# A decoder layer on one core: the position bias moved behind S5's first tables, stores issued by ScalarE, double buffers in the gated unit, and pieces of the merge and of the first FFN products in another order

## The chip, the cores and the metric

The kernel runs on one core of one Trainium2 chip. The metric is the time of one execution in device microseconds. Before the change the median of three runs is 1618.14 us (1615.76 to 1625.18). The profiled execution, from which all rows come, took 1624.46 us.

## What is computed

One layer for a sequence of 1024 tokens with 1024 features, all in float32:

```python
h = rmsnorm(x, norm_mix_g)
u, q, kc_r, vc_r, ks_r, vs_r, kw_r, vw_r, g_nsa, g_br = split(h @ w_in)
y_a = s5_mixer(u, ...) @ w_up_ssm          # recurrence with 64 states per group, then z * sigmoid(z @ w_glu)
kc, vc = compress(kc_r, ...), compress(vc_r, ...)
y_b = nsa_mixer(qh, kc, vc, ks_r, vs_r, kw_r, vw_r, gates, rel_bias) @ w_up_nsa
g_a, g_b = split(sigmoid(g_br))
x = x + (g_a * y_a + g_b * y_b) @ w_out
h = rmsnorm(x, norm_ffn_g)
x = x + (silu(h @ w_ffn_gate) * (h @ w_ffn_up)) @ w_ffn_down
return rmsnorm(x, norm_final_g)
```

The attention adds a position bias of 32 buckets and 8 heads to its logits.

## The kernel before

Every large product is made of three products of 128x512: operands are split into a high part in a reduced format (`wh`, `hhi`, `zh`) and the rest (`wl`, `hlo`, `zl`), and high by high, high by low and low by high are added up in PSUM. The split (`split`, L410) is a cast on ScalarE, GpSimd or VectorE, line 413, 415 or 417, and a subtraction, line 418. Each engine works through its instructions in the order in which the program writes them; that order is the whole schedule. Tiles come from pools with a fixed number of buffers, and a new tile waits until the last user of its buffer is done.

Weights come through `Weights`: two raw buffers (`wr`, loaded by SyncE, L83) and three pairs of split buffers (`wh`, `wl`). `next` (L103) hands out the next unit, and `ahead(2, 4)` splits two and loads four units ahead.

PSUM has the banks "a" (four), "b" and "c" (two each). In attention it is divided anew.

The stages:

1. `head` (L500): the first norm, the transposes of h, the values' projections.
2. `in_proj` (L592), a generator: 28 column blocks of `w_in`, each in two halves of 512 tokens, each half of 8 steps of three products into an "a" bank. What becomes of a bank depends on its kind: "u" (input of S5) goes through eight small copies, "c" (for the compression) and "g" (gates) are copied or passed through the sigmoid by ScalarE (L614, L616), "q" and "k" are split by ScalarE (L607) and VectorE (L608). Then they are stored to DRAM by SyncE (L609, L610, L617). The buffers `evf`, `evh`, `evl` are two each.
3. Beside it runs side work. `along(side, rate)` in `program` takes one piece of the side work (up to its next `yield`) and then `rate` steps of the projections. The side work is, in this order, `s5_params` (rate 4.6), `s5` (3.2), `compress` (3.0) and `glu` (0.8); what is left of the projections comes at the end.
4. `s5_params` (L666) computes the recurrence's parameters in a long chain of small VectorE operations, with the position bias ahead of that chain: 8 products of 128x384 (L712), copies by ScalarE and VectorE, 8 stores. `s5` (L839) works in 8 batches of 4 groups: `tables` on GpSimd and ScalarE (L835, L859), `ways_in` (L873 to L875, giving `w`), `ways_out` (L884 to L890, giving `r`), then transposes, products and a scan.
5. `compress` (L971) loads keys and values (`kk`), eight pieces of 512 KB of its weights (`w1`, L995; three buffers), and multiplies them in groups of 8 small products for each half (L1023). Behind the first three pieces `z_loads` (L1086) loads the input of the gated unit.
6. `glu` (L1057): for each half of the tokens four splits of `z` into `zh` and `zl`, then four products with `w_glu`, a sigmoid (`sg`), a product by VectorE, a split into `ahi` and `alo`.
7. `up_a` (L1093), 16 parts of 12 products, each read from its bank by VectorE (L1110); 12 of them ahead of attention, 4 among its first units. `attention` (L1194) starts a unit (16 rows of a table of due times for each pair of blocks) with `scores` (L1214) and `biased` (L1249).
8. `up_b` and `merge` (L1450): the product with `w_out`, in `units(tiles, half, between)`; each goes over four weight units u, and `between` names what else is written behind or, with "m", in the middle of each u. `square`, `root` and `norm` make the second norm (L1481, L432, L1488), `turned` and `turn("transpose", tile)` its transposes (L469, L1510). For tiles 4 to 7 `turn` also makes sums and differences of the transposed blocks (`sums`, T1, B22, T3, T2, T4; L1517 to L1534).
9. The FFN: `Winograd` replaces each product of 2x2 blocks by seven products of sums of blocks. `pair` (t1 to t4) splits the weights' blocks, `sums` adds them up. `first` (L260) makes the first two weight matrices' products while tiles 6 and 7 are still being normed. Then `run` and the product with `w_ffn_down`.

Of the kernel before, what the change touches and what calls it, by code (L numbers as in the profile page):

```python
# [8 lines left out]
F32 = mybir.dt.float32  # L9
# [7 lines left out]
P = 128  # L17
# [105 lines left out]
class Winograd:  # L123
# [136 lines left out]
    def first(self, norms, turn):  # L260

        V, AC, GP, bank = self.K.nc.vector, self.K.nc.scalar, self.K.nc.gpsimd, self.K.bank
        x0, x1 = self.x[0], self.x[1] = bank("a"), bank("a")
        self.product(0, 1, x0)
        self.product(1, 1, x1)
        next(norms)
        self.t2(0)
        next(norms)  # L270
        self.p1out(0)
        z5 = bank("a")
        self.product(0, 5, z5, half=0)
        turn("transpose", 6, "bc")
        next(norms)
        self.p1out(1)
        turn("sums", 6)
        y = bank("b")
        self.product(0, 6, y, half=0)
        self.product(0, 2, x0, first=False)  # L280
        turn("transpose", 7, "ac")
        turn("T1", 6)
        self.t3(0)
        turn("sums", 7)
        self.product(1, 2, x1, first=False)
        self.p2out(0)
        turn("T1", 7)
        self.t4(0)
        z3, v, c = (bank(t) for t in "abc")
        self.product(0, 3, z3, half=0)  # L290
        self.product(0, 7, v, half=0)
        self.product(0, 4, c, half=0)
        turn("B22", 6)
        turn("B22", 7)
        self.load(2)
        self.product(0, 5, z5, half=1)
        turn("T3", 6)
        turn("T3", 7)
        self.p2out(1)
        self.product(0, 3, z3, half=1)  # L300
        turn("T2", 6)
        turn("T2", 7)
        self.product(0, 7, v, half=1)
        turn("T4", 6)
        turn("T4", 7)
        u2, p5, u3 = self.p.pop(0), self.tile("p1"), self.tile("x11")
        self.product(0, 6, y, half=1)
        self.sums(1, V)
        self.t4(1)
        self.load(3)  # L310
        self.t2(1)
        AC.copy(p5, z5)
        V.tensor_tensor(u2, u2, y, op=OP.add)
        V.tensor_tensor(u3, u2, v, op=OP.add)
        V.tensor_tensor(u2, u2, z3, op=OP.add)
        GP.tensor_tensor(u2, u2, p5, op=OP.add)
        GP.tensor_tensor(p5, u3, p5, op=OP.add)
        self.product(0, 4, c, half=1)
        self.out(0, 1, 1, p5)
        self.out(0, 0, 1, u2)  # L320
        V.tensor_tensor(u3, u3, c, op=OP.add)
        self.out(0, 1, 0, u3)
# [56 lines left out]
class Kernel:  # L379
# [212 lines left out]
    def in_proj(self, specs, ev):  # L592

        nc = self.nc
        for c0, kind, dst in specs:
            w = self.W.next("w_in", 0, KD, c0, P)
            for h in range(2):
# [5 lines left out]
                elif kind in "qk":  # L603
# [5 lines left out]
                    nc.sync.dma_start(dst[0][:, tok], a.bitcast(F32))  # L609
                    nc.sync.dma_start(dst[1][:, tok], b.bitcast(F32))  # L610
                else:
# [5 lines left out]
                    nc.sync.dma_start(dst[:, tok], a)  # L617
# [20 lines left out]
    def s5_loads(self):  # L638
# [22 lines left out]
        self.rb = x("rb", 32, 8)  # L661
        dma(self.rb, A["rel_bias"])
        self.oh = x("oh", 32, 384)
        dma(self.oh, A["consts"][0:32, 874:1258])

    def s5_params(self):  # L666
# [39 lines left out]

        rbb = x("rbb", 32, 8, P)
        V.tensor_copy(rbb, self.rb[:, :, None].to_broadcast([32, 8, P]))
        yield
        for h in range(8):  # L710
            b = self.bank("c")
            nc.tensor.matmul(b[:, 0:384], rbb[:, h, :], self.oh, start=True, stop=True)  # L712
            s = tmp.tile([P, 384], F32, name="brs", tag="brs", bufs=2)
            (AC.copy if h % 2 else V.tensor_copy)(s, b[:, 0:384])
            nc.sync.dma_start(self.bd[h], s)
            yield
# [90 lines left out]
        V.tensor_tensor(self.Bq, self.Bq, w, op=OP.subtract)  # L807

# [29 lines left out]
    def s5(self):  # L838
# [63 lines left out]
        yield  # L902
        zb = None
# [67 lines left out]
    def compress(self, pool):  # L971
# [20 lines left out]
        def w1(j):  # L992
            w = pool.tile([P, 4, 256], F32, name="w1", tag="w1", bufs=3)
# [4 lines left out]
        ws = [w1(j) for j in range(3)]  # L998
# [18 lines left out]
        for which in range(2):  # L1017
            t = self.bank("c")
            for j in range(4):
# [6 lines left out]
                if 4 * which + j < 5:  # L1026
                    ws.append(w1(4 * which + j + 3))
# [29 lines left out]
    def glu(self, pool):  # L1057
        nc, V = self.nc, self.nc.vector
        for h in range(2):
            t = slice(512 * h, 512 * h + 512)  # L1060
            z = self.z[h]
            zs = [pool.tile([P, 4, 512], FR, name=n, tag=n) for n in ("zh", "zl")]
            for k in range(4):
                self.split(zs[0][:, k, :], zs[1][:, k, :], z[:, k, :], "act", "dve")
                yield
            yield
            yield
# [126 lines left out]
    def attention(self, pools, loads, up):  # L1194
# [163 lines left out]
        def start(n):  # L1358
            if n == 2:
# [16 lines left out]
            if n == 1:  # L1376
                run(up, 1)
# [72 lines left out]
    def merge(self, pool, m, td, xd, ffn):  # L1450
# [90 lines left out]
        def units(tts, q, between):  # L1541

            banks = [self.bank("a") for _ in tts]
            for u in range(4):
# [13 lines left out]
                for f, *a in between.get(u, ()):  # L1558
                    f(*a)

        T = lambda tt, *what: [(turn, w, tt) for w in what]
        units((0, 1, 4, 5), 0, {(0, "m"): [(load, tt) for tt in (0, 1, 4, 5)] + [(ffn.factors,)],
# [3 lines left out]
                          1: [(turned, 0)] + T(4, "transpose", "sums"), 2: T(4, "T1", "B22")})  # L1566
# [3 lines left out]
                                (2, "m"): [(load, 6), (load, 7)] + T(5, "T1", "B22"), 2: T(5, "T3", "T2"),  # L1570
                                (3, "m"): T(5, "T4")})
        units((2, 3), 1, {})
# [90 lines left out]
    def program(self):  # L1663
# [25 lines left out]
        self.ut = up.tile([P, G, P], F32, name="ut")  # L1689

# [21 lines left out]
        along(self.s5(), 3.2)  # L1712
        up.release()
# [30 lines left out]
        run(up, 2)  # L1744
# [132 lines left out]
```

## Time and profile before

| | |
|---|---|
| median of three runs | 1618.14 us |
| profiled execution, its own time | 1624.46 us |
| its span, from the first to the last instruction | 1622.7 us |
| TensorE busy | 1561.6 us, 96% |
| VectorE, ScalarE, GpSimd busy | 926.8, 634.6, 637.6 us |
| mean granted TensorE clock | 0.979 of full speed |
| DMA queues' packets | 196.38 MB, mean 121 GB/s |

In the rows PE is TensorE, PEld its weight loads, DVE VectorE, ACT ScalarE, POOL GpSimd and SP SyncE; an engine's name with a q is its queue of DMA issues. L12 is line 12 of the kernel before. Times are microseconds from the span's start. Behind "<-" in square brackets, or after "waited for", stands what ended an engine's idle time, by the semaphores. Ends of matmuls are modelled, and neighbouring ones overlap in the rows.

### The profile page before, as it was taken

What the parts mean: (1) busy time and instruction counts of PE and PEld (TensorE: products, weight loads), DVE (VectorE), ACT (ScalarE), POOL (GpSimd) and SP (SyncE); (2) the same over time, 40 slices, a digit from 0 to 9 for tenths busy, and PEclk for the clock granted to TensorE, in tenths of its full rate; (3) what the DMA queues carried; (4) which work ended last, traced back from release to release, by engine and by line L of the source; (5) the groups of instructions that cost most, each with busy time, mean ns of one, the idle gap of its engine ahead of it and who ended that gap; (6) DMA issues with size and microseconds to landing.
All of it is one profiled execution on the core that took longest, in us unless ns stands there. A gap on an engine that the chain in (4) does not pass through costs nothing. (4 is left out here: it accounts for less than half of the span.)

```text
span 1622.7 us, 22419 instructions
## 1 busy us (share of the span) xinstructions
PE 1561.6 (96%) x7928; PEld 1310.4 (81%) x7928; DVE 926.8 (57%) x1744; ACT 634.6 (39%) x1277; POOL 637.6 (39%) x740
## 2 busy tenths in 40 slices
PE   8998999998999999999999899999999999999995
PEld 8876888886877899998787777888888888888884
DVE  7346886632245899998857564444444445335433
ACT  5212334421220698898116543332333333233322
POOL 1005777610021455555450038677776661000001
PEclk9999999999999999999999989999999999999998
DMA  6342443339337712100666512223222214454551
GB/s 220 107 146 86 123 130 96 94 87 252 98 112 240 203 30 68 42 27 16 217 197 199 176 46 80 89 79 95 81 79 90 79 52 171 150 205 150 177 198 53
DMA packets 165607, 196.38 MB, mean 121 GB/s; under 512 B 20730, under 2 KB 119446, under 8 KB 165495
## 3 DMA queue, kind: packets, MB, share of 16 engines
q1 hardware_dynamic: 165495, 194.94, 38.7%
q8 instruction: 63, 1.03, 0.3%
q14 instruction: 49, 0.40, 0.1%
HBM read 144.96 MB, written 47.84 MB: 119 GB/s over the span
## 5 line engine op out<-in xcount | busy, mean ns | idle before, releaser
L418 DVE TENSOR_TENSOR wl<-wr,wh 128x1024 fp32r<-128x1024 f32 (+1 forms) x170 | 196.8, 1168 | 144.8 <-ACT wh L415 109.6
L406 PE MATMUL a<-hhi,wh 128*128 128x512 f32 x448 | 182.9, 408 | 0.0
L408 PE MATMUL a<-hhi,wl 128*128 128x512 f32 x448 | 178.0, 397 | 0.0
L407 PE MATMUL a<-hlo,wh 128*128 128x512 f32 x448 | 177.8, 397 | 0.0
L415 ACT CAST wh<-wr 128x1024 fp32r<-128x1024 f32 (+1 forms) x138 | 114.4, 844 | 157.2 <-PE a L220 41.6
L1285 POOL TENSOR_SCALAR P<-P,sum,gates 128x640 f32<-128x640 f32 (+3 forms) x192 | 124.8, 663 | 116.6 <-DVE sum L1279 73.5
L219 PE MATMUL a<-mhi,wh 128*128 128x512 f32 (+1 forms) x360 | 139.1, 386 | 2.2 <-ACT wh L415 1.8
L221 PE MATMUL a<-mhi,wl 128*128 128x512 f32 (+1 forms) x360 | 138.7, 385 | 0.8 <-DVE wl L418 0.8
L220 PE MATMUL a<-mlo,wh 128*128 128x512 f32 (+1 forms) x360 | 138.6, 385 | 0.0
L413 POOL TENSOR_SCALAR wh<-wr 128x1024 fp32r<-128x1024 f32 x32 | 34.0, 1064 | 226.8 <-PE a L407 168.8
L160 POOL TENSOR_SCALAR wr<-wr,gcol 128x256 f32<-128x256 f32 x176 | 92.7, 546 | 72.2 <-DVE mlo L474 67.9
L1314 DVE TENSOR_TENSOR PTl<-T,PTh 128x512 fp32r<-128x512 f32 (+3 forms) x200 | 104.2, 544 | 9.7 <-ACT PTh L1313 7.8
L406 PEld LDWEIGHTS a<-hhi,wh 128*128 128x128 f32 x448 | 85.0, 190 | 24.1 <-issue 6.2
L1265 ACT ACTIVATE P<-P,m 128x640 f32<-128x640 f32 (+7 forms) x128 | 95.7, 747 | 17.5 <-DVE m L1249 17.5
L408 PEld LDWEIGHTS a<-hhi,wl 128*128 128x128 f32 x448 | 85.0, 190 | 20.1
L418 DVE TENSOR_TENSOR slo<-sr,shi 128x512 fp32r<-128x512 f32 x44 | 32.0, 728 | 120.0 <-ACT shi L415 120.0
L407 PEld LDWEIGHTS a<-hlo,wh 128*128 128x128 f32 x448 | 85.1, 190 | 17.7
L1313 ACT CAST PTh<-T 128x512 fp32r<-128x512 f32 (+3 forms) x200 | 88.4, 475 | 20.7 <-PE T L1312 19.3
L1249 DVE CUSTOM_DVE_ANT_0 P<-S,B 128x640 f32<-128x640 f32 (+7 forms) x128 | 89.5, 700 | 5.0 <-PE S L1214 2.1
L418 DVE TENSOR_TENSOR wl<-S,wh 128x1024 fp32r<-128x1024 f32 x44 | 65.5, 1489 | 44.4 <-ACT wh L415 41.2
L1312 PE MATMUL T<-cst,P 128*128 128x128 f32 x592 | 87.2, 274 | 3.4 <-DVE PTl L1314 2.8
L415 ACT CAST shi<-sr 128x512 fp32r<-128x512 f32 x44 | 27.1, 619 | 154.4 <-PE c L1638 153.9
(427 smaller groups left out, 3992.1 us busy)
## 6 DMA issues: line engine op xcount, KB each, us to landing
wr<-in_w_ffn_down SPq DMA_DIRECT2D x44, 512.0 KB, 3.4
wr<-in_w_in SPq DMA_DIRECT2D x28, 512.0 KB, 4.1
wr<-in_w_out SPq DMA_DIRECT2D x24, 512.0 KB, 4.3
wr<-in_w_ffn_gate SPq DMA_DIRECT2D x22, 512.0 KB, 3.9
wr<-in_w_ffn_up SPq DMA_DIRECT2D x22, 512.0 KB, 3.7
sr<-sd SPq DMA_DIRECT2D x44, 256.0 KB, 4.0
gd<-evf SPq DMA_DIRECT2D x32, 256.0 KB, 2.6
Q<-qd SPq DMA_DIRECT2D x64, 128.0 KB, 3.0
```

What stands on the lines that cost most here:

```text
L160: self.K.nc.gpsimd.tensor_scalar(t[:, k], t[:, k], self.g[:, 4 * kh + k:4 * kh + k + 1], 1.0, op0=OP.mult, op1=OP.mult)
L219: mm(o, wh[:, k], bh[:, k, c], start=first and k == 0, stop=False, skip_group_check=True)
L220: mm(o, wh[:, k], bl[:, k, c], start=False, stop=False, skip_group_check=True)
L221: mm(o, wl[:, k], bh[:, k, c], start=False, stop=k == 3, skip_group_check=True)
L406: mm(ps, a, c, start=start and k == 0, stop=False, skip_group_check=True)
L407: mm(ps, a, d, start=False, stop=False, skip_group_check=True)
L408: mm(ps, b, c, start=False, stop=stop and k == nk - 1, skip_group_check=True)
L415: nc.scalar.copy(hi, src)
L418: (nc.gpsimd if lo_eng == "pool" else nc.vector).tensor_tensor(lo, src, hi, op=OP.subtract)
L1265: AC.activation(p[:, 0:nk], p[:, 0:nk], AF.Exp, bias=m[:, 0:1], scale=-1.0, accum_out=sm(0))
L1285: sc = lambda x, y, z: GP.tensor_scalar(x, x, a[:, y:y + 1], gate(z), op0=OP.mult, op1=OP.mult)
L1314: V.tensor_tensor(ol, t[:, 0:len(cc), :], oh, op=OP.subtract)
```

## The change

The bias leaves `s5_params` and becomes a generator `bias`, run by `s5` behind `ways_out(0)` and its three empty pieces; all its copies are ScalarE's, and its two inputs get a pool of their own. In `in_proj` the high parts and the undivided blocks are stored by ScalarE, the low parts still by SyncE. The compression gets four weight buffers: four pieces are loaded at the start and one behind each group of the keys. `glu` splits both halves at the start into two sets of buffers, and its two empty pieces go. Two parts of `up_a` move from ahead of attention into it. In `merge` an instruction that needs the square root's table stands at the start; tile 0's and 4's transposes come one weight unit later, and so do T1 and B22 of tile 4; T2 and T4 of tile 5 move into `units((2, 3), 1)`. In `first` t2 goes ahead of the first piece of the norms, tile 7's transposes ahead of the second product, its sums ahead of T1 of tile 6.

```diff
@@ Winograd.first
         self.product(1, 1, x1)
+        self.t2(0)
         next(norms)
-        self.t2(0)
         next(norms)
...
         self.product(0, 6, y, half=0)
+        turn("transpose", 7, "ac")
         self.product(0, 2, x0, first=False)
-        turn("transpose", 7, "ac")
+        turn("sums", 7)
         turn("T1", 6)
         self.t3(0)
-        turn("sums", 7)
         self.product(1, 2, x1, first=False)
+        turn("T1", 7)
         self.p2out(0)
-        turn("T1", 7)
@@ in_proj
-                    nc.sync.dma_start(dst[0][:, tok], a.bitcast(F32))
+                    nc.scalar.dma_start(dst[0][:, tok], a.bitcast(F32))
                     nc.sync.dma_start(dst[1][:, tok], b.bitcast(F32))
...
-                    nc.sync.dma_start(dst[:, tok], a)
+                    nc.scalar.dma_start(dst[:, tok], a)
@@ s5_params (the same products, moved)
-        for h in range(8):
-            b = self.bank("c")
-            nc.tensor.matmul(b[:, 0:384], rbb[:, h, :], self.oh, start=True, stop=True)
-            s = tmp.tile([P, 384], F32, name="brs", tag="brs", bufs=2)
-            (AC.copy if h % 2 else V.tensor_copy)(s, b[:, 0:384])
-            nc.sync.dma_start(self.bd[h], s)
-            yield
+    def bias(self, pool):
+        nc = self.nc
+        rbb = pool.tile([32, 8, P], F32, name="rbb")
+        nc.vector.tensor_copy(rbb, self.rb[:, :, None].to_broadcast([32, 8, P]))
+        yield
+        for h in range(8):
+            b = self.bank("c")
+            nc.tensor.matmul(b[:, 0:384], rbb[:, h, :], self.oh, start=True, stop=True)
+            s = pool.tile([P, 384], F32, name="brs", tag="brs", bufs=2)
+            nc.scalar.copy(s, b[:, 0:384])
+            nc.scalar.dma_start(self.bd[h], s)
+            yield
@@ s5
+        yield from self.bias(self.bs)
         zb = None
@@ compress
-            w = pool.tile([P, 4, 256], F32, name="w1", tag="w1", bufs=3)
+            w = pool.tile([P, 4, 256], F32, name="w1", tag="w1", bufs=4)
...
-        ws = [w1(j) for j in range(3)]
+        ws = [w1(j) for j in range(4)]
...
-                if 4 * which + j < 5:
-                    ws.append(w1(4 * which + j + 3))
+                if which == 0:
+                    ws.append(w1(j + 4))
@@ glu
+        parts = []
+        for h in range(2):
+            parts.append([pool.tile([P, 4, 512], FR, name=n, tag=n, bufs=2) for n in ("zh", "zl")])
+            for k in range(4):
+                self.split(*(x[:, k, :] for x in parts[h]), self.z[h][:, k, :], "act", "dve")
+                yield
         for h in range(2):
             t = slice(512 * h, 512 * h + 512)
-            z = self.z[h]
-            zs = [pool.tile([P, 4, 512], FR, name=n, tag=n) for n in ("zh", "zl")]
-            for k in range(4):
-                self.split(zs[0][:, k, :], zs[1][:, k, :], z[:, k, :], "act", "dve")
-                yield
-            yield
-            yield
+            z, zs = self.z[h], parts[h]
@@ attention, start(n)
-            if n == 2:
+            if n == 3:
                 run(up)
...
-            if n == 1:
+            if n < 3:
                 run(up, 1)
@@ merge
+        one = pool.tile([P, 1], F32, name="one")
+        V.memset(one, 1.0)
+        AC.activation(one, one, AF.Sqrt)
...
-                          1: [(turned, 0)] + T(4, "transpose", "sums"), 2: T(4, "T1", "B22")})
+                          2: [(turned, 0)] + T(4, "transpose", "sums"), (3, "m"): T(4, "T1", "B22")})
...
-                                (2, "m"): [(load, 6), (load, 7)] + T(5, "T1", "B22"), 2: T(5, "T3", "T2"),
-                                (3, "m"): T(5, "T4")})
-        units((2, 3), 1, {})
+                                (2, "m"): [(load, 6), (load, 7)] + T(5, "T1", "B22"), 2: T(5, "T3")})
+        units((2, 3), 1, {0: T(5, "T2"), 1: T(5, "T4")})
@@ program
         make_bias(0)
-        run(up, 2)
```

Three places in the engines' order, before and after. First SyncE's queue at the start of the compression (`kk` its inputs, `w1` its weights, `z` the gated unit's input, `gd` the gates in DRAM, `wr` raw weights). Before:

```order
L986 DMA kk_3179<-cd_62 64x1008
L995 DMA w1_3184<-in_cmp_w1_k 64x4x256 x2
L995 DMA w1_3187<-in_cmp_w1_k 64x4x256 x2
L995 DMA w1_3190<-in_cmp_w1_k 64x4x256 x2
L1086 DMA z_3193<-zd_64 128x512 x4
L1086 DMA z_3198<-zd_64 128x512 x4
L617 DMA gd_63<-evf_3209 128x512
L617 DMA gd_63<-evf_3237 128x512
L83 DMA wr_3244<-in_ssm_w_glu 128x4x256
L617 DMA gd_63<-evf_3276 128x512
L617 DMA gd_63<-evf_3308 128x512
L83 DMA wr_3315<-in_w_in 128x8x128
```

and its next row is `w1_3339`, the fourth piece. With the change:

```order
L991 DMA kk_3131<-cd_62 64x1008
L1000 DMA w1_3136<-in_cmp_w1_k 64x4x256 x2
L1000 DMA w1_3139<-in_cmp_w1_k 64x4x256 x2
L1000 DMA w1_3142<-in_cmp_w1_k 64x4x256 x2
L1000 DMA w1_3145<-in_cmp_w1_k 64x4x256 x2
L1091 DMA z_3148<-zd_64 128x512 x4
L1091 DMA z_3153<-zd_64 128x512 x4
L83 DMA wr_3189<-in_w_in 128x8x128
L83 DMA wr_3258<-in_ssm_w_glu 128x4x256
L1000 DMA w1_3290<-in_cmp_w1_v 64x4x256 x2
```

The fourth piece stands ahead of the z loads, the gate stores have left this queue, and the values' first piece (`w1_3290`) follows two weight loads.

Second ScalarE in `merge`, at the norms of tiles 0 and 4 (`xn` the normed tile, `wh` the third weight unit of `units((1, 5), 1)` and its neighbours, `mhi` the transposed high parts). Before:

```order
L415 CAST wh_8922<-wr_8890 128x1024
L1481 ACTIVATE xn_8931,ss_8930<-x1_8721 128x1024
L1481 ACTIVATE xn_8942,ss_8941<-x1_8725 128x1024
L432 ACT_TABLE_LOAD
L432 ACTIVATE rstd_8944<-ss_8930,eps_103 128x1
L415 CAST wh_8958<-wr_8908 128x1024
L1488 ACTIVATE xn_8931<-x1_8721,rstd_8944 128x1024
L432 ACTIVATE rstd_8965<-ss_8941,eps_103 128x1
L1488 ACTIVATE xn_8942<-x1_8725,rstd_8965 128x1024
L415 CAST wh_8984<-wr_8926 128x1024
L473 CAST mhi_8241<-b_8996 128x4x128
```

With the change:

```order
L415 CAST wh_8929<-wr_8897 128x1024
L1486 ACTIVATE xn_8938,ss_8937<-x1_8728 128x1024
L1486 ACTIVATE xn_8949,ss_8948<-x1_8732 128x1024
L432 ACTIVATE rstd_8951<-ss_8937,eps_103 128x1
L415 CAST wh_8965<-wr_8915 128x1024
L1493 ACTIVATE xn_8938<-x1_8728,rstd_8951 128x1024
L432 ACTIVATE rstd_8972<-ss_8948,eps_103 128x1
L1493 ACTIVATE xn_8949<-x1_8732,rstd_8972 128x1024
L415 CAST wh_8991<-wr_8933 128x1024
L415 CAST wh_9009<-wr_8969 128x1024
L473 CAST mhi_8245<-b_9021 128x4x128
```

The table load is gone from here (it stands thirteen rows up, at the merge's start), and one more weight cast stands ahead of the transposes' first casts.

Third ScalarE in `first` (`S` the weights' sums for t2 and t3, `xn` the norms of tiles 6 and 7, `p1` copies of the first two products, `b22` and `t1` sums of tiles 6 and 7). Before:

```order
L1481 ACTIVATE xn_9519,ss_9518<-x1_9211 128x1024
L432 ACTIVATE rstd_9521<-ss_9518,eps_103 128x1
L415 CAST wh_9527<-S_8855 128x1024
L1488 ACTIVATE xn_9519<-x1_9211,rstd_9521 128x1024
L1481 ACTIVATE xn_9533,ss_9532<-x1_9213 128x1024
L432 ACTIVATE rstd_9535<-ss_9532,eps_103 128x1
L234 COPY p1_9541<-a_9492 128x512
L1488 ACTIVATE xn_9533<-x1_9213,rstd_9535 128x1024
L234 COPY p1_9567<-a_9493 128x512
L1517 COPY b22_9569<-c_9557 128x512
L415 CAST mhi_8241<-t1_9570 128x4x128
L415 CAST wh_9613<-S_8855 128x1024
```

With the change:

```order
L415 CAST wh_9525<-S_8862 128x1024
L1486 ACTIVATE xn_9530,ss_9529<-x1_9218 128x1024
L432 ACTIVATE rstd_9532<-ss_9529,eps_103 128x1
L1493 ACTIVATE xn_9530<-x1_9218,rstd_9532 128x1024
L1486 ACTIVATE xn_9540,ss_9539<-x1_9220 128x1024
L432 ACTIVATE rstd_9542<-ss_9539,eps_103 128x1
L234 COPY p1_9548<-a_9499 128x512
L1493 ACTIVATE xn_9540<-x1_9220,rstd_9542 128x1024
L234 COPY p1_9574<-a_9500 128x512
L1522 COPY b22_9576<-c_9564 128x512
L1522 COPY b22_9618<-c_9597 128x512
L415 CAST mhi_8245<-t1_9577 128x4x128
```

t2's cast (`wh_9525`) stands ahead of tile 6's square, and tile 7's copy (`b22_9618`) ahead of the cast for T1 of tile 6 and of the one for t3, which is the next row.

## Rows read from the trace of the kernel before

**Rows 1.** The page: span, and busy time of each engine.

```profile
span 1622.7 us, 22419 instructions
PE 1561.6 (96%) x7928; PEld 1310.4 (81%) x7928; DVE 926.8 (57%) x1744; ACT 634.6 (39%) x1277; POOL 637.6 (39%) x740
```

**Rows 2.** TensorE's waits over the span: total us, times, longest.

```profile
PE b L912 <- DVE w L875: 3.3, 2, 2.5
PE c L219 <- ACT T2h L415: 3.1, 1, 3.1
PE a L406 <- ACT zh L415: 2.7, 1, 2.7
PE S L1214 <- DVE m L1249: 2.3, 3, 1.2
PE a L1468 <- DVE x L1474: 2.2, 1, 2.2
PE a L219 <- ACT wh L415: 1.8, 1, 1.8
```

**Rows 3.** Stretches: length, each engine's busy us (instructions), granted clock, DMA share, GB/s.

```profile
140.00:160.00 20.00, 14.52 (x69) 10.71 (x68) 10.43 (x12) 4.62 (x8) 15.54 (x13) 1.00 0.26 81
...
398.58:402.21 3.63, 3.63 (x17) 3.63 (x18) 0.00 (x0) 0.00 (x0) 0.00 (x0) 0.50 1.07 273
456.90:460.30 3.40, 3.40 (x10) 2.62 (x9) 2.24 (x3) 0.54 (x2) 0.00 (x0) 0.51 0.70 279
860.20:866.40 6.20, 6.15 (x22) 5.27 (x23) 3.94 (x10) 4.71 (x7) 0.00 (x0) 0.50 0.42 110
955.90:962.00 6.10, 5.93 (x19) 5.06 (x20) 5.46 (x7) 2.02 (x3) 3.80 (x2) 0.50 0.17 38
1100.00:1120.00 20.00, 20.00 (x90) 16.55 (x89) 9.49 (x11) 6.92 (x11) 14.62 (x16) 1.00 0.11 29
```

**Rows 4.** Timeline, S5's start: start, length, engine, instruction, [idle before <- ended by].

```profile
147.50 0.69 DVE L875 TENSOR_TENSOR w<-m,m 128x512 f32<-128x512 f32 x1 [9.80 <-POOL m L874]
...
146.47 0.63 ACT L859 ACTIVATE sn<-xt 128x512 f32<-128x512 f32 x1 [17.98 <-POOL xt L835]
```

**Rows 5.** Timeline, compression: SyncE's issues, then TensorE's groups of weights.

```profile
375.86 8.71 SPq L1086 DMA_DIRECT2D z<-zd  x8
...
390.70 0.98 SPq L617 DMA_DIRECT2D gd<-evf  x2
...
392.29 1.33 SPq L995 DMA_DIRECT2D w<-in_cmp_w_k  x2
...
379.41 2.02 PE L1023 MATMUL c<-kv,w 128*128 128x126 f32 x16 [0.18 <-DMA w<-in_cmp_w_k]
...
398.58 3.76 PE L1023 MATMUL c<-kv,w 128*128 128x126 f32 x16 [7.30 <-DMA w<-in_cmp_w_k]
```

**Rows 6.** A stretch of 2 us among the z loads, columns as in rows 3.

```profile
388.00:390.00 2.00, 2.00 (x16) 1.83 (x15) 0.00 (x0) 0.00 (x0) 0.00 (x0) 1.00 1.05 391
```

**Rows 7.** Timeline of VectorE, end of the gated unit's first half.

```profile
449.63 1.23 DVE L418 TENSOR_TENSOR wl<-wr,wh 128x1024 fp32r<-128x1024 f32 x1 [6.71 <-POOL wh L413]
```

**Rows 8.** Timeline, merge: TensorE, ScalarE, VectorE.

```profile
860.19 1.12 PE L469 MATMUL b<-cst,xn 128*128 128x128 f32 x4 [2.91 <-ACT xn L1488]
...
856.57 1.28 ACT L432 ACT_TABLE_LOAD   x1
...
859.12 1.22 DVE L418 TENSOR_TENSOR wl<-wr,wh 128x1024 fp32r<-128x1024 f32 x1 [0.32 <-ACT wh L415]
...
895.66 2.47 DVE L1474 TENSOR_TENSOR x<-x,a 128x512 f32<-128x512 f32 x4
```

**Rows 9.** Timeline, first products of the FFN: ScalarE, then VectorE.

```profile
938.60 1.06 ACT L415 CAST wh<-S 128x1024 fp32r<-128x1024 f32 x1 [2.89 <-PE a L220]
...
955.25 0.62 ACT L415 CAST T2h<-t 128x512 fp32r<-128x512 f32 x1 [2.09 <-DVE t L1534]
...
940.84 0.68 DVE L1518 TENSOR_TENSOR t<-a,mhi 128x512 f32<-128x512 f32 x1
```

More of the change, by code (lines that the diff above doesn't have):

```diff
@@ L660, in s5_loads @@
         dma(self.dd, A["ssm_d"].rearrange("(g c) -> g c", c=16))
[L661 to L664, printed above, removed]
     def s5_params(self):
@@ L705, in s5_params @@
         yield
-        rbb = x("rbb", 32, 8, P)
-        V.tensor_copy(rbb, self.rb[:, :, None].to_broadcast([32, 8, P]))
-        yield
-        for h in range(8):
-            b = self.bank("c")
-            nc.tensor.matmul(b[:, 0:384], rbb[:, h, :], self.oh, start=True, stop=True)
-            s = tmp.tile([P, 384], F32, name="brs", tag="brs", bufs=2)
-            (AC.copy if h % 2 else V.tensor_copy)(s, b[:, 0:384])
-            nc.sync.dma_start(self.bd[h], s)
-            yield
         are, aim = q[:, 0:32], q[:, 32:64]
@@ L807, in s5_params, with bias_loads @@
         V.tensor_tensor(self.Bq, self.Bq, w, op=OP.subtract)
+    def bias_loads(self, pool):
+        self.rb, self.oh = pool.tile([32, 8], F32, name="rb"), pool.tile([32, 384], F32, name="oh")
+        self.nc.sync.dma_start(self.rb, self.A["rel_bias"])
+        self.nc.sync.dma_start(self.oh, self.A["consts"][0:32, 874:1258])
+    def bias(self, pool):
[10 more added lines that the diff above has]
+            yield
     def exp(self, out, x, pool, name, n):
@@ L1058, in glu @@
         nc, V = self.nc, self.nc.vector
+        parts = []
[4 more added lines that the diff above has]
+                yield
         for h in range(2):
             t = slice(512 * h, 512 * h + 512)
-            z = self.z[h]
-            zs = [pool.tile([P, 4, 512], FR, name=n, tag=n) for n in ("zh", "zl")]
-            for k in range(4):
-                self.split(zs[0][:, k, :], zs[1][:, k, :], z[:, k, :], "act", "dve")
-                yield
-            yield
-            yield
+            z, zs = self.z[h], parts[h]
             for n in range(2):
@@ L1689, in program @@
         self.ut = up.tile([P, G, P], F32, name="ut")
+        self.bs = self.pool("bs", side="right")
+        self.bias_loads(self.bs)
         specs = [(P * i, "u", i) for i in range(4)]
@@ L1712, in program @@
         along(self.s5(), 3.2)
+        self.bs.release()
         up.release()
```

## The prediction

> **What bounds the kernel now.** I read the page's engine table first: TensorE is busy for 1561.6 us of a span of 1622.7 us [rows 1]. The change removes no product, so it can only win back part of the 61 us in which TensorE stands still, and part of what its clock loses after a standstill. Second, the list of TensorE's waits [rows 2]: it names what ended each standstill, with the total. These are between 1.8 and 3.3 us, each ended by one operation of ScalarE or VectorE; one of 7.3 us for the compression's weights, a DMA, and one of 2.9 us in the merge stand with their surroundings under b and e. Third, the stretches with the granted clock [rows 3]. At full clock 90 products of 512 columns take 20 us, 0.22 us each, so a projection step of three is 0.67 us. Behind six of these waits the clock stood at half (1.2 GHz); four of the stretches stand there, and those behind the waits for x and for wh (L219) have the form of the one at 456.9, 3.4 us. A busy stretch at half clock costs half its length, and such a loss goes only if the wait before it goes. The S5 waits (5.5 us missing in the row of 140 to 160 us) were followed by none: a wait of this size may cost the clock or not.
>
> **The sum** is made against the profiled execution's 1624.46 us. The median of the three runs is 1618.14 us, 6.3 us lower; I carry the difference over unchanged.
>
> **a. Bias behind S5's first tables.** The 8 products, 8 copies and 8 stores stay; they change place. Before, they stand ahead of the parameter chain of VectorE, and TensorE reaches S5's first transposes too early: w is late because VectorE waits 9.8 us for GpSimd's part, which queues behind the first tables [rows 4]. Now the parameter chain starts 41 projection steps earlier (9 pieces x 4.6), and 9 pieces with 3.2 steps each, 28.8 x 0.67 = 19 us, stand between the tables and the first transposes. 19 us of new cover against 5.5 us missing: all 5.5 us go. Late next would be ScalarE: it waits 18.0 us for GpSimd's table [rows 4], and the four "a" banks, each 8 steps or 5.4 us long, last for 21 us, so 3 us are left. Lower end: 2.
>
> **b. Stores on ScalarE, four buffers for the compression's weights.** SyncE issued the fourth piece of the key weights at 392.3 us, behind the z loads and behind gate stores that waited for their copies [rows 5]; TensorE had been waiting since 391.3 (398.58 less 7.30) and went on at 398.6. Now that piece goes out ahead of the z loads, and the stores no longer stand in SyncE's queue. The first piece for the values can leave once the z loads have been issued (384.6 us, and 2.2 us for the two issues more, at the z loads' 1.09 us each). With the 6.3 us from issue to use of the late piece it is there at 393 to 394, and TensorE gets to it at 395.3 (391.3, a group of 2.0 us and three steps). I take the whole: 7.3 us of wait, and half of the 3.63 us at half clock behind it, together 9.1 us; lower end 3.0 (below).
> ScalarE's price: 56 stores (48 of the projections, 8 of the bias). The trace shows none issued there. The nearest row is SyncE's own: 0.49 us each for gate stores, 1.09 us each for z loads on a crowded queue [rows 5]. I take 0.49, nearest because it is the same store: 27 us of ScalarE's time over the whole stage of the projections; ScalarE is 39% busy over the span [rows 1] and each bank has three others in reserve, so nothing on the path. The other end is 1.09 x 56 = 61 us, all on the path (a rival). A store waiting for its own copy holds up ScalarE's next copy, for which the "a" bank and TensorE wait; that is the place where it would show.
> A rule speaks against this part. At 388 to 390 us the DMA engines were fully busy (share 1.05, 391 GB/s) [rows 6]: a queue that is full does not empty faster because someone else fills it. The Trainium skill, page "DMA: Bandwidth & Descriptors", section "Issuing engines are not separate DMA queues", says that DMAs started by different engines run on the same 16 DMA engines, and that only the issuing time is saved. By it, b would come down to the first rival's 3.0 and the sum to 20.4. The trace bears out both readings: the engines were full, and the issue at 392.3 came 11 us after the first group had left its buffer at 381.4 [rows 5].
>
> **c. Double buffers in the gated unit.** The casts of the second half were queued behind sg's chain, VectorE there waiting 6.7 us for GpSimd [rows 7], and TensorE waited 2.7 us for zh [rows 2], then 3.4 us at half clock: 2.7 + 1.7 = 4.4 us. Both halves are now cast before the first product. Six pieces of cover between the halves go as well: the weights of the projection next in line take the buffer that the first half's last products free, 9 products (2 us) ahead of their use, with a cast on GpSimd and 1.2 us on VectorE between; I deduct 0.6. Gain 3.8, ends 2.9 and 4.4.
>
> **d. Start of attention.** Six parts of the up-projection instead of four lie among the first scores, so units 0 to 2 have been scored when this cover ends. Of the 2.3 us for m [rows 2] I take 1.2. The value loads are issued no earlier while their use comes a microsecond earlier: ends -1 and 2.3.
>
> **e. Merge, tile 0.** TensorE waits 2.9 us for the normed tile [rows 8], from 857.3 on; ScalarE had loaded the square root's table for 1.28 us just before. That load now lies at the merge's start, where ScalarE waits for DMAs anyway, and the transposes come one unit (12 products, 2.7 us) later. But the third unit's weights are then late: their low part, right behind the high one, started at 859.12 [rows 8], now 1.28 us earlier at 857.8, and ends 1.2 us later. TensorE comes there at 857.3, waits 0.5 us for the high part, does one product and waits 1.0 us more for the low part. About 1.6 us of wait remain; gain 1.3. The 6.2 us at half clock behind it may stay; upper end 2.9 + 3.1 = 6.0, lower end 0.
>
> **f. Tile 5's T2 and T4.** TensorE waits 2.2 us for the additions that free its banks; they ran at 895.66, behind these pieces [rows 8]. With the pieces behind two later units the additions follow their products directly; ScalarE and VectorE are then idle enough. 2.2 us and half of 3.4 us at half clock (the same form as the row of c): 3.9, lower end 2.2.
>
> **g. First products of the FFN.** t2 ahead of the norms removes most of the 1.8 us for wh, but the norms come later, by 0.3 us as I estimate, since VectorE does t2's low part (1.2 us, as in [rows 8]) ahead of theirs, and the transposes wait for them. What ends the stage is the chain to tile 7's T4 at 955.25, for which TensorE waits 3.1 us [rows 2, 9]. Now the three sums of tile 7 (0.68 us each, 2.0 us) fall into the time in which ScalarE waits 2.9 us for a weight buffer [rows 9]. Chain earlier by 2.0 - 0.3 = 1.7, and as TensorE comes earlier too, the wait stays and with it the half clock. Gain 1.7, ends -1 and 7.9 (all waits, and half of the 5.9 us at half clock).
>
> 5.5 + 9.1 + 3.8 + 1.2 + 1.3 + 3.9 + 1.7 = **26.5 us**: 1598 for the profiled execution, 1592 on the scale of the median. All upper ends give 39 us (1579), all lower ends 8 us (1610).
>
> **The rivals.** First: the compression is bound by the DMA engines, not by SyncE's order. The additional piece (0.5 MB, 1.3 us at 391 GB/s) delays what is behind it, and the values' first piece takes the place in the full queue that the fourth piece had: it is there as late, at 398.6 and 1 us more, while TensorE comes at 395.3; 4.3 us of wait and 1.8 us of clock stay, b is 3.0, time 1598. For it: share 1.05 [rows 6]; against: the issue that came late.
> Second: waits that move on. c to g are chains of two engines that were hidden behind a longer wait; if each is replaced by the next link, only a and b are won, 14.6 us, time 1603. For it: e and g already show it in my working; against: f and c remove work from the chain.
> Third, the change doesn't do what it says in S5: ScalarE stands behind the sine table, the four banks fill up, and TensorE waits for a bank instead of for w. a is 0, time 1597. It decides when ScalarE's wait is longer than 21 us.
> Fourth, slower: ScalarE's stores. Each holds ScalarE until its copy has been written and for the issue; if over 34.6 us of the 56 stores' time, 0.62 us each, fall on TensorE's path, the kernel is slower by over 0.5%. At 1.09 us each, 61 us, the time is 1653. Against it: ScalarE's 39% in the table [rows 1].
>
> **How the numbers follow.** Forecast 0.48; with full clock in e and g as well (1580) 0.07; first rival 0.14, second 0.12, third 0.06; first and second together (1618.1 - 8.5, about 1610) 0.08, counted as no change; slower 0.05. The range 1578 to 1610 reaches from all upper ends, with 1 us for the median's spread, to all lower ends. 0.5% (8 us) is about what a measurement of this kernel can tell from no change. Faster 0.87, within 0.5% 0.08, slower 0.05.
>
> **What would show it.** Right: no wait of TensorE between S5's tables and its first batch; the compression's products without a wait over 2 us; no wait for zh; a wait of 1 to 2 us for wh instead of xn near the merge's tile 0; none for x; still about 3 us for T2h, and half clock behind it. Wrong: waits of TensorE for "a" banks (copies of ScalarE) in the projections, a wait of over 4 us for the compression's value weights, or TensorE's busy time above 1562 us by more than the clock explains.

## The result, and the profile after

The change made the kernel slower. It takes 1630.92 us (median of 6 runs, 1628.56 to 1633.85), the kernel before beside it 1619.96 us (6 runs): ratio 1.0070, 95% interval 1.0049 to 1.0091, 11 us more. The forecast was 1592 us. The profiled execution took 1628.56 us, the fastest of the six, while that of the kernel before (1624.46 us) is near the upper end of its runs, so the two profiles lie closer together than the medians.

The page of the kernel after, against [rows 1]:

```profile
span 1626.8 us, 22398 instructions
PE 1555.9 (96%) x7928; PEld 1306.2 (80%) x7928; DVE 913.7 (56%) x1741; ACT 635.6 (39%) x1281; POOL 640.0 (39%) x740
```

TensorE makes the same 7928 products in 5.7 us less busy time, so fewer of them ran at half clock, but the span is 4.1 us longer: it stands still for 9.8 us longer (70.9 against 61.1 us). Its list of waits, against [rows 2]:

```profile
PE c L807 <- DVE rbb L803: 13.1, 1, 13.1
PE c L1028 <- DMA w<-in_cmp_w_v: 7.6, 1, 7.6
PE a L1473 <- DVE x L1479: 3.2, 1, 3.2
PE c L219 <- ACT T2h L415: 3.1, 1, 3.1
...
PE a L408 <- DVE wl L418: 1.5, 1, 1.5
...
PE S L1219 <- DVE m L1254: 1.3, 3, 0.7
PE a L1473 <- ACT wh L415: 1.3, 1, 1.3
```

Of the six rows of [rows 2], S5's w, the gated unit's zh and the wh of L219 are gone; T2h stands as before, m has fallen from 2.3 to 1.3 us, and x has grown from 2.2 to 3.2 us in another place (877 instead of 894 us). The compression's 7.3 us for key weights [rows 5] has become 7.6 us for value weights. New, and larger than everything else, is one wait of 13.1 us: the first of the moved bias products (L807) waits for `rbb`, the copy of the bias table that VectorE spreads over 128 columns. VectorE's timeline there:

```profile
98.77 0.69 DVE L877 TENSOR_TENSOR m<-pr,Bp 128x512 f32<-128x512 f32 x1
109.27 0.69 DVE L879 TENSOR_TENSOR w<-m,m 128x512 f32<-128x512 f32 x1 [9.81 <-POOL m L878]
...
111.64 1.52 DVE L879 TENSOR_TENSOR w<-m,m 128x512 f32<-128x512 f32 x1 [0.95 <-POOL m L878]
...
121.79 0.67 DVE L803 COPY rbb<-rb 32x1024 f32<-32x1024 f32 x1
```

The wait for GpSimd of [rows 4], 9.80 us, is here again with 9.81 us. `rbb` needs nothing of it, but is written behind it, and behind w, r and two weight splits; it comes at 121.8 us, while TensorE had been standing since 109.4. The wait for GpSimd ends at 109.3 us, just as TensorE stops: what TensorE waits for is the work that this wait had held up on VectorE, which is busy for 11.0 of the 13.1 us. The stretches with the granted clock, against [rows 3] (length, busy us of each engine, clock, DMA share, GB/s):

```profile
109.40:122.50 13.10, 0.00 (x0) 0.00 (x0) 10.99 (x18) 2.48 (x11) 6.30 (x5) 0.64 0.20 49
122.50:133.40 10.90, 10.88 (x22) 6.63 (x23) 1.23 (x1) 1.54 (x3) 1.04 (x1) 0.50 0.44 147
403.58:406.50 2.92, 2.92 (x14) 2.92 (x15) 0.00 (x0) 0.00 (x0) 0.00 (x0) 0.50 1.08 278
833.20:836.60 3.40, 3.40 (x10) 2.63 (x9) 0.25 (x1) 0.10 (x1) 0.00 (x0) 0.50 0.76 235
881.00:884.40 3.40, 3.40 (x9) 2.63 (x9) 1.32 (x6) 3.40 (x7) 0.00 (x0) 0.50 0.98 386
959.50:966.30 6.80, 5.86 (x19) 4.98 (x20) 5.49 (x8) 2.67 (x4) 3.80 (x2) 0.50 0.11 25
```

Behind the 13.1 us the clock stood at half (1.2 GHz) for 10.9 busy us, a loss of 5.5 us more.

### The profile page after: what moved, and what is told of

Same layout as the page of the kernel before. It is cut to its first block, busy times and chain, and to the rows that moved or that the text cites. A ratio compares the mean times of both kernels' runs of the same rounds, so it can differ in the third digit from the quotient of the medians.

```text
span 1626.8 us, 22398 instructions
## 1 busy us (share of the span) xinstructions
PE 1555.9 (96%) x7928; PEld 1306.2 (80%) x7928; DVE 913.7 (56%) x1741; ACT 635.6 (39%) x1281; POOL 640.0 (39%) x740
## 5 line engine op out<-in xcount | busy, mean ns | idle before, releaser
L408 PE MATMUL a<-hhi,wl 128*128 128x512 f32 x448 | 178.8, 399 | 1.5 <-DVE wl L418 1.5
L219 PE MATMUL a<-mhi,wh 128*128 128x512 f32 (+1 forms) x360 | 138.7, 385 | 0.4 <-ACT p L234 0.3
L408 PEld LDWEIGHTS a<-hhi,wl 128*128 128x128 f32 x448 | 85.4, 191 | 22.1 <-DVE wl L418 2.0
L1254 DVE CUSTOM_DVE_ANT_0 P<-S,B 128x640 f32<-128x640 f32 (+7 forms) x128 | 89.5, 699 | 2.9 <-PE T L1317 1.3
```

Source lines behind the costliest of these rows:

```text
L219: mm(o, wh[:, k], bh[:, k, c], start=first and k == 0, stop=False, skip_group_check=True)
L408: mm(ps, b, c, start=False, stop=stop and k == nk - 1, skip_group_check=True)
```

## The experiments

All ratios are to the kernel before on the same chip, with 95% intervals; a thousandth is 1.6 us. The kernel before took 1621.9 to 1623.4 us (medians) beside these runs, 2 to 3.5 us more than beside the change; the change itself was not run again beside them. A difference between two of these runs, or between one of them and the change, is the difference of their ratios.

### The place of the bias and of rbb

`e1_rbb_early` writes one copy earlier, `e2_bias_back` takes the whole of part a back:

```diff
 (e1_rbb_early, s5)
+        self.rbb = self.bs.tile([32, 8, P], F32, name="rbb")
+        V.tensor_copy(self.rbb, self.rb[:, :, None].to_broadcast([32, 8, P]))
         tables(0)
 (bias)
-        nc.vector.tensor_copy(rbb, self.rb[:, :, None].to_broadcast([32, 8, P]))
 (e2_bias_back, s5; and the bias in s5_params as before)
-        yield from self.bias(self.bs)
```

> The change with one edit: the copy of the bias table (rbb) on VectorE stands ahead of S5's first tables, all else as in the change. Theory (rbb's place): the 13.1 us wait of the first bias product and about 5.5 us at half clock behind it go, 1631 - 18.6 = about 1612 us, and no wait of over 1 us takes their place up to S5's first batch. Rival 1 (ScalarE: the bias copies stand behind the sine tables and fill the banks): the wait comes back on ScalarE, 1625 to 1631 us. Rival 2 (w itself is late): TensorE waits 3 to 8 us for w instead, 1617 to 1622 us.

Measured: 1.0006 (0.9995 to 1.0018). Against the change's 1.0070 one copy of 0.67 us, moved, is worth 10 us, give or take 4; expected were 18.6. The 13.1 us are gone, but TensorE, now earlier, meets waits that the list of the change doesn't have, two of them shown here, and a longer one for the value weights:

```profile
PE c L1029 <- DMA w<-in_cmp_w_v: 8.4, 1, 8.4
...
PE c L961 <- DMA tz<-kz: 2.1, 1, 2.1
...
PE a L406 <- POOL m L888: 1.4, 1, 1.4
```

The 1.4 us at 115.7 us stand ahead of a projection's product, whose weight GpSimd casts behind the first tables and w's products; by the profile that cast ends at 115.3 us, and the row names GpSimd's next product, so what lasts until 117.1 us stays open. The 2.1 us at 214.3 are for `tz`, a DMA of SyncE that waited 4.5 us for ScalarE's store of `kd`. Each is followed by 3.4 us at half clock.

> The change with its part a undone: bias products, copies and stores back ahead of the parameter chain as in the kernel before; the rest as in the change. Theory (rbb's place): the 18.6 us go and the 5.5 us of waits for w, r and wt of the kernel before come back, about 1618 us. So the rest of the change would be worth about 2 us against the kernel before. Rival (the stores of ScalarE cost the path, all over the projections): only 2 to 5 us less than the change, 1626 to 1629 us.

Measured: 0.9971 (0.9959 to 0.9984), 1617.8 us, as the theory had it. Part a as a whole costs 9.9 thousandths, 16 us: 10 for rbb's place (give or take 4), 6 for the rest (give or take 3). The change without part a is 5 us faster than the kernel before, where the prediction had 21.

### The stores

`e3_stores_sync` and `f1_bias_back_stores_sync` give the stores back to SyncE in e1 (all 56) and in e2 (the projections' 48); `g2_stores_alone` gives the 48 to ScalarE in the kernel before:

```diff
-                    nc.scalar.dma_start(dst[:, tok], a)
+                    nc.sync.dma_start(dst[:, tok], a)
```

> e1_rbb_early with all 56 stores back on SyncE. Theory: a store on ScalarE costs TensorE nothing, so nothing is won by taking it away; in the compression SyncE has the stores in its queue again and the weights come 0 to 3 us later: e1 + 0 to 4 us, 1612 to 1616 us. Rival (ScalarE's stores are on the path, 0.33 us each or more): 5 to 18 us faster than e1, 1594 to 1607 us.

Measured: 1.0005 (0.9992 to 1.0019), as e1. The bias stores in SyncE's queue make TensorE wait 5.9 us for ScalarE's copies of the bias; against that the 2.1 us for `tz` are gone and the wait for the value weights is 3.7 us instead of 8.4. That the stores' place did the last is not shown: `f1_bias_back_stores_sync` and `f4_merge_mended` below, on one chip, have 6.6 us for the value weights with the stores on SyncE and 6.9 with them on ScalarE.

> e2_bias_back (the bias back ahead of the parameter chain) with the projections' 48 stores back on SyncE as well; four weight buffers kept. Theory (slots): with the stores on ScalarE, SyncE's loads wait for the completion of a store that ScalarE has not yet issued, so taking them back costs nothing and the compression gets shorter by 2 to 6 us; 1612 to 1616 us where e2_bias_back has 1618 us. Rival (issuing on ScalarE frees SyncE, as the prediction had it): the gate stores' waits for copies return to SyncE's queue, the weights come later, 1619 to 1623 us.

Measured: 0.9971 (0.9958 to 0.9983), 1617.7 us, e2's time to a tenth. Neither side's number came: the stores' place makes no difference.

> The kernel before with the projections' 48 stores issued by ScalarE, nothing else. Theory (slots): SyncE waits for the stores' completion where it waited for the copies, and ScalarE's 0.33 us each are covered: ratio 0.998 to 1.002. The prediction's b: up to 9 us faster with its four buffers, some of it here, 0.995 to 0.997. The prediction's fourth rival: slower, 1.005 and more.

Measured: 1.0003 (0.9992 to 1.0015). Three pairs agree: no gain and no loss in the sum. Why no gain is to be seen in SyncE's waits from 345 to 412 us. Kernel before:

```profile
SPq L617 <- ACT evf L614: 18.7, 5, 9.1
```

The change:

```profile
SPq L1000 <- DMA gd<-evf: 5.4, 1, 5.4
SPq L1091 <- DMA gd<-evf: 5.1, 1, 5.1
...
SPq L991 <- DMA gd<-evf: 3.6, 1, 3.6
```

SyncE no longer waits for the copy that a gate store needs. It waits, ahead of its own loads of `kk` (L991), weights (L1000) and z (L1091), for the gate stores themselves to land; `g2_stores_alone` has the same three waits, 5.1, 6.3 and 3.6 us, ahead of `kk`, weights and z. The program's waits say how: the DMAs of SyncE and ScalarE share eight completion semaphores in turn, and the next user of one waits until the last has landed, as here the second `kk` load, whose semaphore was last used by a gate store of ScalarE:

```
205 L990 DMA kk_3126<-cd_62 64x1008
206 L991 DMA kk_3126<-cd_62 64x1008 [waits DMAHW3_49]
```

A store that ScalarE issues only when its copy is done holds such a semaphore all that time. That the trace names a store as what ended these waits is shown; that the semaphores cost what the stores won follows from the equal times only, no run changed their number.

### Buffers and order in the compression

`h1_four_buffers_alone` is the kernel before with four buffers; `e4_z_late` (on e1) and `f2_bias_back_z_late` (on e2) move the z loads:

```diff
 (h1_four_buffers_alone)
-        ws = [w1(j) for j in range(3)]
+        ws = [w1(j) for j in range(4)]
 (e4_z_late, f2_bias_back_z_late; z_loads in program is gone)
                     ws.append(w1(j + 4))
+                    if j == 3:
+                        self.z_loads()
```

> The kernel before with part b's other half alone: four buffers for the compression's weights, the fourth piece issued ahead of the z loads and the values' pieces behind them; stores stay on SyncE. Theory (order in a full queue): the 7.3 us wait for the fourth key piece goes, and a wait of 4 to 8 us for the first value piece, now behind the eight z loads, takes its place: ratio 0.998 to 1.001. The prediction's b: 0.994 to 0.996.

Measured: 1.0004 (0.9993 to 1.0015). The 7.3 us for the fourth key piece went, and 7.3 us for the first value piece came. In its list of TensorE's waits:

```profile
PE c L1023 <- DMA w<-in_cmp_w_v: 7.3, 1, 7.3
```

and in SyncE's timeline:

```profile
376.13 8.86 SPq L1086 DMA_DIRECT2D z<-zd  x8
...
393.60 2.66 SPq L995 DMA_DIRECT2D w<-in_cmp_w_v  x4
```

> e1_rbb_early with the eight z loads issued behind the last piece of the values' weights instead of ahead of the first. Theory (order in a full queue): the first piece for the values is issued about 10 us earlier, its wait of 7.6 us and 1.5 us of half clock behind it go, and z (used 30 us later) still arrives in time: e1 - 9 us, about 1603 us. Rival (the DMA engines bound the compression whatever the order): a wait of 4 to 8 us stays for the weights or shows up for zh in the gated unit: within 3 us of e1, 1609 to 1615 us.

Measured: 0.9949 (0.9934 to 0.9965), 5.7 thousandths or 9.2 us below e1, as expected to a few tenths. The value weights are issued at 376.8 us, z behind them; of the compression's waits 1.4 us is left (1.2 for key and 0.2 for value weights), and none for zh came:

```profile
376.81 11.91 SPq L1001 DMA_DIRECT2D w<-in_cmp_w_v  x8
389.31 11.15 SPq L1094 DMA_DIRECT2D z<-zd  x8
```

The eight value loads now take 11.9 us to issue, 1.5 us each, where the z loads of [rows 5] took 1.09: the queue is no emptier than before, only the bytes needed first go first.

> e2_bias_back with the z loads behind the last piece of the values' weights (as e4_z_late). Theory (order in a full queue): the wait of 3.9 us for the values' weights and up to 3 us of half clock behind it go, the 2.3 us for the key weights stay: 1611 to 1614 us. Rival (DMA engines bound it): within 2 us of e2_bias_back, 1616 to 1620 us.

Measured: 0.9938 (0.9918 to 0.9958), 1611.9 us, in the theory's range.

### The gated unit

`g1_glu_alone` is the kernel before with the new `glu`, whose diff stands above.

> The kernel before with part c alone (both halves of the gated unit cast ahead, two buffers each). Theory (the 2.7 us wait for zh and 1.7 us of half clock go, nothing takes their place but about 0.6 us): 3 to 5 us faster than the kernel before, ratio 0.997 to 0.998. Rival (waits move on to the next projection's weights): ratio 0.999 to 1.001.

Measured: 0.9977 (0.9964 to 0.9990), 3.7 us faster; the wait for zh is not in its list and no other took its place in the gated unit.

### The merge and the first products

`h2_merge_parts_alone` is the kernel before with parts e, f and g, `h4_tile5_alone` with f alone (both in the change's diff). `f4_merge_mended` takes e2 and mends two places:

```diff
-        V.memset(one, 1.0)
-        AC.activation(one, one, AF.Sqrt)
+        AC.activation(one, self.eps, AF.Sqrt)
...
-                          2: [(turned, 0)] + T(4, "transpose", "sums"), (3, "m"): T(4, "T1", "B22")})
+                          2: [(turned, 0)] + T(4, "transpose", "sums"), 3: T(4, "T1", "B22")})
```

> The kernel before with parts e, f and g alone (Sqrt early, tile 4 one unit later, tile 5's T2 and T4 later, tile 7's sums earlier). Theory (waits move on): the waits for xn, x at 894 us and wh go, 1.4 and 0.8 us at the merge's start, 3 us for x in front of tile 4's pieces and 1.2 to 1.5 us for xn come: ratio 0.997 to 1.000. The prediction's e to g, 6.9 us: 0.995 to 0.997.

Measured: 0.9996 (0.9982 to 1.0010). The waits in its list, where [rows 2, 8] have 2.9 for xn, 2.2 for x and 1.8 for wh:

```profile
PE a L1468 <- DVE x L1474: 3.3, 1, 3.3
...
PE a L1468 <- ACT wh L415: 1.6, 2, 1.4
PE b L469 <- ACT xn L1488: 1.6, 1, 1.6
PE a L1469 <- DVE wl L418: 1.5, 2, 0.8
```

xn and x have moved, wh now stands at the merge's start, and the low parts (wl) have come. The one for x can be read in the kernel after: T1 and B22 of tile 4, one unit later than before, now stand ahead of the additions (L1479) of their unit group, and TensorE wanted a bank from 877.6 us on:

```profile
877.70 1.22 DVE L418 TENSOR_TENSOR wl<-wr,wh 128x1024 fp32r<-128x1024 f32 x1
878.84 0.68 DVE L418 TENSOR_TENSOR mlo<-t,mhi 128x512 fp32r<-128x512 f32 x1
879.44 0.68 DVE L418 TENSOR_TENSOR mlo<-b,mhi 128x512 fp32r<-128x512 f32 x1
880.04 1.27 DVE L1479 TENSOR_TENSOR x<-x,a 128x512 f32<-128x512 f32 x2
```

The one for wh is ScalarE's early table load: the Sqrt reads a tile that VectorE sets (L1568) behind a wait for GpSimd, and the merge's first weight cast stands behind both:

```profile
828.50 0.06 DVE L1568 MEMSET one<- 128x1 f32 x1 [1.44 <-POOL mlo L418]
...
828.62 1.28 ACT L1569 ACT_TABLE_LOAD   x1 [22.18 <-DVE one L1568]
829.92 0.20 ACT L1569 ACTIVATE one<-one 128x1 f32<-128x1 f32 x1
830.03 1.98 ACT L415 CAST wh<-wr 128x1024 fp32r<-128x1024 f32 x2
```

ScalarE had been idle for 22 us before.

> The kernel before with part f alone (T2 and T4 of tile 5 behind two later units). The prediction's f, 3.9 us (2.2 us of wait for x and 1.7 us of half clock go): 0.997 to 0.998. Rival (the wait moves on, to the norms or the next weights): 0.999 to 1.001.

Measured: 0.9985 (0.9970 to 0.9999), 2.4 us faster: the wait for x is gone, as forecast, and 1.3 us for xn at 907.7 us and 0.7 us more for wh came. As e, f and g together give 0.6 us, e and g together would cost about 2, which by the difference, with an interval of 3 us either way, is not clear of nothing.

> e2_bias_back with two edits in the merge: the Sqrt that loads the table early reads the constant tile eps instead of a tile that VectorE has to set first, and T1 and B22 of tile 4 stand behind the additions of the third unit group's last unit instead of ahead of them. Theory (each of the two new waits has its own cause in the written order): the waits of 1.35 and 0.76 us at the merge's start and of 2.9 us for x go, with up to 3 us of half clock: 1611 to 1614 us where e2_bias_back has 1618 us. Rival (the merge's chain of ScalarE and VectorE is full, waits move on): the waits come back for T3, T2 or the norms, 1616 to 1620 us.

Measured: 0.9970 (0.9955 to 0.9986), e2's 0.9971: no gain. The 1.35 us at the start are gone, but x is waited for 2.2 and 1.8 us at 833 and 863 us, where e2 has 1.2 and 2.9. Mending single links moved the waits again. One thing more can be read here. Up to the merge, at about 800 us, the two programs are the same, and yet the wait for the value weights at about 400 us differs by 3 us, first e2, then this run:

```profile
PE c L1022 <- DMA w<-in_cmp_w_v: 3.9, 1, 3.9
...
PE c L1022 <- DMA w<-in_cmp_w_v: 6.9, 1, 6.9
```

They ran on different chips; whether that or the single execution made the difference is not shown. A change of this wait by 3 us between two profiles is no proof of an edit's effect.

### S5's start, and the parts together

`g5_ways_in_first` (on e2) swaps two pieces. `h6_cover_and_z_late` is f2 with three empty pieces more ahead of the first batch, and f4's Sqrt. `f3_all_mended` is f1 with z late and f4's edits; `g6_best` is f2 with g5's swap, f4's Sqrt, and the values' half of kk loaded and added up later.

```diff
 (g5_ways_in_first)
-        tables(0)
-        yield
         ways_in(0)
         yield
+        tables(0)
+        yield
 (g6_best, compress; the sum of kk's second half follows two pieces later)
-        ks = [keys(0), keys(1)]
+        ks = [keys(0)]
...
         ws = [w1(j) for j in range(4)]
+        ks.append(keys(1))
 (h6_cover_and_z_late)
         ways_out(0)
+        yield
+        yield
+        yield
```

> e2_bias_back with ways_in(0) written ahead of tables(0) in S5's start, so that GpSimd multiplies w's second part before the tables and not 10 us later. Theory (GpSimd's queue order makes w late): the waits of 0.8 and 2.5 us for w at the first batch and the half clock behind them go, 4 to 6 us: 1612 to 1614 us where e2_bias_back has 1618 us. Rival (the tables are then late for the scan's input, the wait moves on by one step): within 2 us of e2_bias_back.

Measured: 0.9988 (0.9976 to 1.0001), 2.8 us slower than e2, with an interval of 3 us, so not clear of e2's time; the 4 to 6 us of the theory did not come. w is in time, and r, the next product on GpSimd behind the tables, is not:

```profile
PE c L918 <- DVE r L885: 5.8, 1, 5.8
```

> f2_bias_back_z_late with ways_in first (as g5_ways_in_first), the values' half of kk loaded behind the key weights and added up two pieces later, and the Sqrt of f4_merge_mended. Theory: f2's 1612 us less 4 to 6 us in S5, 3 to 6 us for the key weights, 1 to 2 us at the merge's start: 1599 to 1604 us, ratio 0.986 to 0.989. Rival (waits move on): 1608 to 1612 us.

Measured: 0.9946 (0.9928 to 0.9965), 1614.5 us, no better than f2 and slower than either expectation: it has g5's wait for r, and no wait for key weights but 5.4 us for the value weights.

> f1_bias_back_stores_sync with z late and the two edits of f4_merge_mended. Theory: what is won by each adds up, 1600 to 1605 us, 15 us or more below the kernel before. Rival (waits move on): 1608 to 1614 us.

Measured: 0.9932 (0.9912 to 0.9952), 1611.3 us, in the rival's range: what each edit had won or was to win did not add up.

> f2_bias_back_z_late with three pieces more between S5's first tables and its first batch (9.6 projection steps, 6.4 us, taken from the end of the projections), and the Sqrt of f4_merge_mended. Theory (what S5's start lacks is cover, and the bias products are not needed for it): the 4 us of waits for w and wt and 1.7 us of half clock go, 1605 to 1608 us on the scale on which f2 has 1612 us, ratio 0.989 to 0.991. Rival (waits move on, as in g5_ways_in_first): 0.993 to 0.995.

Measured: 0.9918 (0.9897 to 0.9940), 1607.8 us, the lowest median of all: 13 us below the kernel before, 25 below the change. The ratio lies between the two expectations, and its interval reaches into both; against f2 it is 3 us, with an interval of 5. Its page and the first of its waits in S5 and the compression:

```profile
span 1603.2 us, 22422 instructions
PE 1546.2 (96%) x7928; PEld 1297.4 (81%) x7928; DVE 921.6 (57%) x1744; ACT 635.4 (40%) x1279; POOL 637.7 (40%) x740
```

```profile
PE c L1025 <- DMA w<-in_cmp_w_k: 1.7, 1, 1.7
...
PE b L933 <- DVE wt L915: 1.4, 1, 1.4
```

With plain projection steps as cover the waits for w, 3.3 us in f2, are gone; 1.4 us for wt stay. That the time of the kernel fell by it is likely but not clear of noise.

## Why the prediction was wrong

**a, the step that failed most.** The prediction priced the cover (19 us) and asked who else might be late: ScalarE behind the sine table. It didn't place the one VectorE instruction that the cover itself needs. The step "9 pieces with 3.2 steps each stand between the tables and the first transposes" counts the first of these pieces, `rbb`, as cover, though it stands on VectorE behind the very wait of 9.8 us [rows 4] that it was to cover, and behind the work held up by it. TensorE needs `rbb` only one piece of 3.2 steps behind the place where the transposes had stood. The cover itself did its part: in the change's list there is no wait for w. But a was not +5.5, it was -16 us: 10 by that copy (e1), 6 by the rest (e1 against e2). For the rest the cause is in part open: e1's list has waits that e2's has not, for `tz`, for GpSimd and more for the value weights, and no run takes them apart. The third rival looked at the right place, S5's tables, and named the wrong engine.

**b, forecast 9.1, measured nothing** (g2: -0.5 us, h1: -0.6 us, each give or take 2 us; beside four buffers the stores' place made no difference either, e2 against f1). The first rival was right in kind and not bold enough: it left 3.0 us of gain, h1 none. The step "The first piece for the values can leave once the z loads have been issued", at 386.8 us, took SyncE's rate of issue as fixed; in the change the z loads took until 391.9 us, the value weights were issued at 393.1, and from issue to use they took 10.5 us and not 6.3. The prediction's own sign of being wrong, a wait of over 4 us for the value weights, came: 7.6 us. That the engines were full [rows 6] was the better row. The Trainium skill, page "DMA: Bandwidth & Descriptors", section "Issuing engines are not separate DMA queues", has the rule that another issuing engine saves only the time of issuing; g2's 1.0003 agrees with it. The fourth rival's price is answered too: ScalarE's stores took 0.33 us each in the trace (forecast 0.49), and the three pairs show no net cost; the one place where a store of ScalarE reaches TensorE in the lists above is e1's wait for `tz`.

**c, forecast 3.8, measured 3.7** (g1). The chain was right: the wait and the half clock behind it went. The prediction's deduction, the next projection's weights, is the 1.5 us for wl (L408) in the change's list; g1 has none there.

**d, forecast 1.2.** It was not run alone. In the lists the waits for m (L1254) fell from 2.3 to 1.3 us.

**e, f, g, forecast 6.9, measured 0.6** (h2). f's mechanism was right, 2.4 us of the 3.9 (h4). In e, the forecast held at tile 0 itself, where 0.7 us are left of 2.9 in the change, but two steps failed elsewhere: the Sqrt at the merge's start was put "where ScalarE waits for DMAs anyway", but it waited for a memset of VectorE, which waited for GpSimd; and tile 4's T1 and B22 were not followed to the additions that they now precede. In g, T2h's 3.1 us stayed, as forecast; no run has g alone, so whether its 1.7 us came is not shown. The second rival, waits that move on, describes e to g; with b's loss as well the prediction had 1610, and the 21 us from there to 1631 are a's swing from +5.5 to -16.

**The slower rival** was the wrong mechanism. The parts, -16 and -1 us for a and b, +3.7 for c, +0.6 for e to g and about +1 for d by the lists alone, give 12 us slower against 11 measured. As a is itself the difference between the change and e2, this tests b to g only: 4.3 us in parts, 4.7 together.

## What to carry to other kernels

A block that is moved to cover a wait must not itself begin with work for an engine that is in that wait: look up, for each of its instructions, what stands ahead of it in its own engine's queue. In a full DMA queue the question is which bytes go first, not which engine issues them: putting late-needed loads behind early-needed ones won 5 to 9 us, a further buffer and another issuing engine nothing. Where TensorE is 96% busy and the others follow closely, price a removed wait only after naming the next link; the plainest cover, more of the main work ahead of it, had the lowest time here (h6), though not clear of the run without it.

## What was not expected of the hardware

The same wait doesn't always cost the same clock: the T2h wait of 3.1 us was followed by 3.4 us at half clock in e1 and by 6.8 us in the change and in e4, in the same place of the program. Added up over the stretches at half clock, h6 has 10 busy us in all, the change 36, h2 25 and the kernel before 45. e2 and f4, the same program up to the merge, have 25 and 17 busy us at half clock up to 780 us. Two profiles of the same work can so differ by a few us of TensorE's busy time, and gains of that size need many runs, not two traces.
